# Modulation columns of two chunks summed on VectorE in the head of a two-layer mixer kernel, and conditioning rows made once

## The chip, the cores and the metric

One core of a Trainium2 chip runs the whole program. The metric is the device time of one execution in microseconds (us), the median of several runs. In the profile PE is TensorE's matmul, PEld its weight load, ACT ScalarE, DVE VectorE, POOL GpSimd, and SP the engine that issues most loads; a "q" behind an engine is its instruction queue.

## What is computed

Two layers of a mixer for 384 tokens (128 context tokens, group 0, and 256 latent tokens, group 1) of width 2048, all in float32. Each layer first makes a modulation vector for each group from a conditioning vector, then modulates the normalised input, and then runs projections, attention, a gated MLP, a pooling branch, merge gates and an output projection. Cut to what matters here:

```python
mod_ctx = silu(c_ctx) @ w_ada[l] + b_ada[l]          # 2048 -> 3 * 2048, group 0
mod_lat = silu(c) @ w_ada[l] + b_ada[l]              # the same for group 1
shift, scale, gate = jnp.split(mod, 3, axis=-1)
h = rmsnorm(x, norm_w) * (1.0 + scale) + shift
q, k, v, ga, u, vb, gb, z, gc = split_cols(h @ w_in) # everything else starts from h
```

## The kernel before

Activations lie transposed: 128 channels on the partitions, 384 tokens along the row; a chunk is 128 of the 2048 channels, so a layer has 16 chunks of `h`. A float32 product is made of three fast products: each operand is a rounded high half and the rest (low half). For weights ScalarE rounds the high half `H` (line 75) and VectorE subtracts to get the low half `L` (line 76); for chunks of `h`, ScalarE makes the high half (line 469) and VectorE recomputes and subtracts (lines 470 and 471).

**The stream.** All weights come as 674 tiles of 128 x 1024 (512 KB), in an order that the kernel writes out by hand. Each is an `Item`: it is loaded by SP (line 197), split (`do_split`), multiplied (`mm`), and followed by `post`. `run_items` walks the list; each engine gets its instructions in the order in which this walk issues them, and works them off in that order.

**The head** is the first 92 items of layer 0 (`n_wide`). It has six blocks of token strips `kv` (18 matmuls for two chunks, line 299; here named kv3, kv4 for block 3, kv5, kv6 for block 4), of `t_part` items (24 matmuls, lines 954 to 956, whose results VectorE adds up in line 967), and of modulation items. A modulation strip (`ada_strip`, n chunks wide) multiplies the conditioning columns by `w_ada` on TensorE (line 355) into PSUM; ScalarE copies the result (line 361), TensorE turns it (line 372), and VectorE sums and adds the bias (lines 373 to 380). `ada_pair(c, n)` is the strips of scale and shift for chunks c to c + n - 1. `h` of a chunk can be made only when its pair is done. `nexts` and `SPREAD` say which strips of the next block stand ahead of which item of a block. With n = 4 a strip takes 8 items of 2 matmuls of 512 columns; with n = 2, 4 items of 4 matmuls of 256 columns. The profile records each of these matmuls twice.

In the head an item's split is issued at most two items ahead, and only if at most two splits are open:

```python
while i < n_wide and sp <= i + 2 and sp < loaded[0] and inflight + items[sp].split <= ahead_split:
    if not do_split(items[sp], sp <= i + 1):
        break
```

**Columns on VectorE.** `ada_col` is the other way to get a modulation column: two tiles of transposed `w_ada`, each multiplied with the conditioning row of a group, spread over all partitions in `sB`, and summed by one VectorE instruction (line 399). Layer 0's gates and layer 1's columns are made like this, after the head. The two sums of an item go to the list `lowq`; one is issued after each item with a split, and those of an item that has passed at once:

```python
while lowq and lowq[0][0].idx < i:
    lowq.pop(0)[1]()
...
if it.split and lowq:
    lowq.pop(0)[1]()
```

**Conditioning rows.** `load_cond` (called at item 6 of the part behind the head) loads both rows, spread over 128 partitions, into the four `sb` buffers with POOL's DMA queue. `spread_cond` then applies SiLU to all of it in eight pieces (lines 126 to 128).

**Buffers.** In the head, modulation tiles take one of four `sb` buffers, or else one of up to nine `u` buffers; all other tiles take one of six `raw` buffers (`load_upto`). The SP queue loads in the order of the list, so a tile without a free buffer holds up those behind it. Line 600 scales x by its norm, in parts, at fixed items (26, 48 and 70).

Of the kernel before, what the change touches and what calls it, by code (L numbers as in the profile page):

```python
# [8 lines left out]
F32 = mybir.dt.float32  # L9
F32R = mybir.dt.float32r  # L10
I32 = mybir.dt.int32
AF = mybir.ActivationFunctionType
ALU = mybir.AluOpType
AX = mybir.AxisListType

P = 128
D = 2048
# [12 lines left out]
def hybrid_kernel(ctx: ExitStack, tc: tile.TileContext, x_t, cond_t, cond, vecs_t, cache_kt, cache_v, w_stream,  # L30
                  q_norm_w, k_norm_w, sgu_pool_t, b_sgu, rope_tab, edge_tab, y_t, state_k, state_v, order):
    nc = tc.nc
    PE, ACT, DVE, POOL, SP = nc.tensor, nc.scalar, nc.vector, nc.gpsimd, nc.sync
# [14 lines left out]
    def nm(s):  # L48
        uid[0] += 1
        return f"{s}_{uid[0]}"  # L50

    def unit(dt=F32, shape=(P, 4, T)):
        return big.tile(list(shape), dt, tag="u6", name=nm("u"))

    def s2(shape=(P, 512)):
        return mid.tile(list(shape), F32, tag="s2", name=nm("s"))

    def sm(n):
        return small.tile([P, 16], F32, tag="sm", name=nm("m"))[:, :n]
# [34 lines left out]
    def load_vectors():  # L94
        raw = s2((P, 128))
        SP.dma_start(raw[:, 0:32], cond_t)
        cl = const.tile([P, 2, P], F32, name="cols")
        for l in range(DEPTH):
            v = cl[:, l, :]
            cols.append(dict(norm=v[:, 0:16], ada=v[:, 16:64], merge=v[:, 64:112], pscale=v[:, 112:116],  # L100
                             sguw=v[:, 116:120], fin=v[:, 120:128]))
        sg = s2((P, 128))
        ACT.activation(sg[:, 0:32], raw[:, 0:32], AF.Tanh, scale=0.5)
        DVE.tensor_scalar(sg[:, 0:32], sg[:, 0:32], 0.5, 0.5, ALU.mult, ALU.add)
        for g in range(2):
            DVE.tensor_tensor(scT[:, :, g], sg[:, 16 * g:16 * g + 16], raw[:, 16 * g:16 * g + 16], ALU.mult)
        def vec_load():
            SP.dma_start(cl[:], vecs_t)

        def halve():  # L110
            for c in cols:
                DVE.tensor_scalar(c["merge"], c["merge"], 0.5, None, ALU.mult)
        after(halve, 10)
        ACT.activation(sm(1), eps[:], AF.Ln)
        return vec_load

# [2 lines left out]
    sB = {}  # L119
    scrap = const.tile([P, 1024], mybir.dt.bfloat16, name="scrap")  # L120

    def spread_cond():
        def chunk(g, q):
            sl = sB[g, q // 2][:, (q % 2) * 512:(q % 2 + 1) * 512]
            sg = s2()
            ACT.activation(sg[:], sl, AF.Tanh, scale=0.5)
            DVE.tensor_scalar(sg[:], sg[:], 0.5, 0.5, ALU.mult, ALU.add)
            DVE.tensor_tensor(sl, sl, sg[:], ALU.mult)
        return [lambda g=g, q=q: chunk(g, q) for q in range(4) for g in range(2)]

    def load_cond():
        for g in range(2):
            for hf in range(2):
                sB[g, hf] = sbp.tile([P, 1024], F32, tag="sb", name=nm("sb"))
                POOL.dma_start(sB[g, hf][:], cond[g, hf * 1024:(hf + 1) * 1024].partition_broadcast(P))
    xt_dram = [x_t, tc.dram_tile([4, P, 4, T], F32, name="xt")]


    items = []
# [4 lines left out]
    def after(fn, delay=1):  # L144
        later.setdefault(pos[0] + delay, []).append(fn)
# [21 lines left out]
    loaded = [0]  # L167
    lowq = []
# [3 lines left out]
    def midpoint():  # L172
        while midq:
            midq.pop(0)()

    held = {"sb": 0, "u": 0, "raw": 0}

    def load_upto(n, first=False):
        while loaded[0] < min(n, len(items)):
            it = items[loaded[0]]  # L180
            if it.wide:
                kind = "sb" if first and held["sb"] < 4 else "u"
            else:
                kind = "raw"
            if first and held[kind] >= {"sb": 4, "u": 9, "raw": 6}[kind]:
                return
            held[kind] += 1
            it.kind = kind
            loaded[0] += 1
            if kind == "sb":  # L190
                it.raw = sbp.tile([P, 1024], F32, tag="sb", name=nm("sb"))
            elif kind == "u":
                it.raw = unit(shape=(P, 1024))
            else:
                it.raw = wraw.tile([P, 1024], F32, tag="raw", name=nm("raw"))
            n_col = it.srcs[-1][1]
            SP.dma_start(it.raw[:, :n_col], w_stream[len(order), :, :n_col])
            order.append(it.srcs)
# [18 lines left out]
    def run_items(n_wide, wide_ahead, ahead=5, ahead_split=2):  # L217
# [4 lines left out]
        for i in range(n):  # L222
            while lowq and lowq[0][0].idx < i:
                lowq.pop(0)[1]()
            if i < n_wide:
                load_upto(min(i + 1 + wide_ahead, n_wide + ahead), True)
            else:
                load_upto(i + 1 + ahead)
# [161 lines left out]
    def ada_col(l, c):  # L390
        def mk(hf):
            def pre(it):
                for g in range(2):
                    lowq.append((it, lambda g=g: step(it, g)))

            def step(it, g):
                m = mods[l][:, c, g:g + 1]
                init, dst = ((cols[l]["ada"][:, c:c + 1], part[:, c, g:g + 1]), (part[:, c, g:g + 1], m))[hf]
                DVE.tensor_tensor_reduce(scrap[:], it.raw[:], sB[g, hf][:], 1.0, init,  # L399
                                         ALU.mult, ALU.add, dst)  # L400
                if hf and g:
                    have.add((l, c))
                    if c >= 32:
                        mm = mods[l][:, c, :]
                        DVE.tensor_scalar(mm, mm, 0.25, None, ALU.mult)
                    if 16 <= c < 32:
                        mm = mods[l][:, c, :]
                        DVE.scalar_tensor_tensor(
                            mm, mm, 1.0, cols[l]["norm"][:, c - 16:c - 15].to_broadcast([P, 2]), ALU.add, ALU.mult)
            return pre  # L410

        return [Item([(0, 1024, ("w_ada_t", l), 8 * hf, 8, c * P, P)], pre=mk(hf), split=False) for hf in range(2)]
# [604 lines left out]
    head_a, rest_a = layer(0)  # L1017
# [3 lines left out]
    def ada_pair(c, n):  # L1021
        return ada_strip(0, 16 + c, n) + ada_strip(0, c, n)

    items += ada_pair(0, 1)
    nexts = [ada_pair(1, 1), ada_pair(2, 2)] + [ada_pair(4 * g, 4) for g in range(1, 4)] + [[]]
    SPREAD = [[2, 2, 0], [0, 0, 8], [0, 4, 4, 8], [4, 4, 4, 4, 0, 0], [4, 4, 4, 4, 0, 0], [0, 0, 0, 0, 0, 0]]
    for b in range(6):
        nxt, blk = nexts[b], head_a[b]
        for j, it in enumerate(blk):
            m = SPREAD[b][j]  # L1030
            items += nxt[:m]
            nxt = nxt[m:]
            items.append(it)
        items += nxt
# [1 line left out]
    extra = gate0 + [it for c in range(16) for o in (0, 16) for it in ada_col(1, c + o)]  # L1036
    body, left = mix(rest_a, extra, 2, 20)
    assert not left
    rest_a[6].before = load_cond
    rest_a[12].before = lambda: lowq.extend((rest_a[40], fn) for fn in spread_cond())  # L1040
    items += body
    items += ada_strip(1, 32, 4, 5) + ada_strip(1, 36, 2, 2)
    items += head_b
# [2 lines left out]
    assert not left  # L1046
    items += body
    vec_load = load_vectors()
    xT0 = load_x()
    vec_load()  # L1050
    load_upto(8, True)
    sum_x(xT0)
    run_items(n_wide, 24)
# [75 lines left out]
```

## Time and profile before

| | before |
|---|---|
| median of 3 runs (lowest to highest) | 2159.76 us (2159.47 to 2160.26) |
| the profiled execution | 2159.66 us, span 2157.9 us |
| granted TensorE clock, mean | 0.997 |
| TensorE busy | 2136.8 us (99%) |
| VectorE busy | 1290.1 us (60%) |
| ScalarE busy | 790.9 us (37%) |
| share of the chain that ended last | TensorE 99%, VectorE 1% |
| TensorE line 355 (modulation strips) in that chain | 2% |
| DMA moved | 375.60 MB |

The span runs from the first to the last instruction of the trace; the time is that of the whole execution. The chain is followed back from the last instruction, at each step to what released it. A line that is idle elsewhere costs nothing as long as it is not in this chain.

### The profile page before, as it was taken

The page shows a single profiled execution, that of the slowest core. Times are in us where ns is not written, and L with a number is a line of the kernel's source. Part 1 is how long each engine was busy: PE and PEld are TensorE (multiplying, and loading weights), DVE is VectorE, ACT ScalarE, POOL GpSimd, SP SyncE. Part 2 cuts the span into 40 slices and gives each one's busy share as a digit, 9 for nine tenths or more (in the row PEclk, how much of TensorE's full clock was granted, in tenths as well). Part 3 has the DMA queues.
Part 4 walks back from the last instruction along what each step waited for, and adds up shares of the span by engine and source line. Part 5 has one row for each costly group of instructions (what it writes and reads, how often), then busy time and mean ns, then how long its engine had stood idle before and what let it go on. Part 6 is the DMA issues. An engine that isn't in the chain of part 4 may idle for free.

```text
span 2157.9 us, 30028 instructions
## 1 busy us (share of the span) xinstructions
PE 2136.8 (99%) x12102; PEld 2027.6 (94%) x12102; DVE 1290.1 (60%) x2015; ACT 790.9 (37%) x1137; POOL 22.6 (1%) x70
## 2 busy tenths in 40 slices
PE   8999999999999999999999999999999999999997
PEld 6789898989999999999988889999999999999997
DVE  6566775757667876767767676753443444443444
ACT  4242445453323333333344345453232333332432
POOL 0000000000000000000000000000000000000000
PEclk9999999999999999999999999999999999999998
DMA  9965354545555565567774553443333333334531
GB/s 383 409 216 187 119 185 148 175 143 183 197 190 184 189 196 188 184 200 240 254 256 142 163 165 128 161 143 108 127 125 129 127 127 127 126 126 135 176 128 72
DMA packets 104461, 375.60 MB, mean 174 GB/s; under 512 B 11937, under 2 KB 13473, under 8 KB 104321
## 3 DMA queue, kind: packets, MB, share of 16 engines
q1 hardware_dynamic: 101056, 359.66, 49.4%
q0 software_dynamic: 3264, 14.03, 2.1%
q8 instruction: 94, 1.54, 0.3%
q14 instruction: 47, 0.38, 0.1%
HBM read 366.82 MB, written 6.82 MB: 173 GB/s over the span
## 4 chain that ended last, share of the span: by engine, by line
PE 99%; DVE 1%; ACT 0%; DMA 0%; issue 0%; DVEq 0%; SPq 0%
PE b L336 26%; PE b L334 26%; PE b L335 26%; PE b L279 3%; PE b L278 3%; PE b L277 3%; PE b L299 3%; PE b L355 2%; PE b L954 1%; PE b L562 1%; PE b L542 1%; PE b L956 1%; PE b L955 1%; PE b L553 1%; PE b L589 0%; DVE u L1014 0%
## 5 line engine op out<-in xcount | busy, mean ns | idle before, releaser
L334 PE MATMUL b<-u,H 128*128 128x384 f32 x3184 | 1075.7, 338 | 0.0
L336 PE MATMUL b<-u,L 128*128 128x384 f32 x3184 | 1064.2, 334 | 0.0
L335 PE MATMUL b<-u,H 128*128 128x384 f32 x3184 | 1063.9, 334 | 0.0
L76 DVE TENSOR_TENSOR L<-raw,H 128x1024 fp32r<-128x1024 f32 (+1 forms) x481 | 587.0, 1221 | 638.1 <-ACT H L75 638.0
L75 ACT ACTIVATE H<-raw 128x1024 fp32r<-128x1024 f32 (+1 forms) x481 | 507.2, 1055 | 838.0 <-PE b L335 686.4
L335 PEld LDWEIGHTS b<-u,H 128*128 128x128 f32 x3184 | 597.9, 188 | 4.5 <-issue 1.0
L334 PEld LDWEIGHTS b<-u,H 128*128 128x128 f32 x3184 | 597.9, 188 | 4.5 <-issue 1.0
L336 PEld LDWEIGHTS b<-u,L 128*128 128x128 f32 x3184 | 597.7, 188 | 0.0
L399 DVE CUSTOM_DVE_ANT_0 scrap<-raw,sb,part 128x1024 bf16<-128x1024 f32 x116 | 148.2, 1277 | 0.0
L399 DVE CUSTOM_DVE_ANT_0 scrap<-raw,sb,cols 128x1024 bf16<-128x1024 f32 x116 | 148.1, 1276 | 0.0
L277 PE MATMUL b<-H,u 128*128 128x512 f32 x288 | 115.1, 400 | 0.0
L279 PE MATMUL b<-H,u 128*128 128x512 f32 x288 | 112.4, 390 | 0.0
L278 PE MATMUL b<-L,u 128*128 128x512 f32 x288 | 112.2, 390 | 0.0
L832 ACT ACTIVATE s<-b,cols 128x384 f32<-128x384 f32 x96 | 55.6, 581 | 114.4 <-PE b L336 114.4
L278 PEld LDWEIGHTS b<-L,u 128*128 128x128 f32 x288 | 54.1, 188 | 11.8
L277 PEld LDWEIGHTS b<-H,u 128*128 128x128 f32 x288 | 54.1, 188 | 11.7
L279 PEld LDWEIGHTS b<-H,u 128*128 128x128 f32 x288 | 54.0, 188 | 11.5
L299 PE MATMUL b<-H,u 128*128 128x512 f32 x192 | 52.8, 397 | 0.2 <-DVE u L471 0.2
L954 PE MATMUL b<-u,H 128*128 128x384 f32 x144 | 49.7, 345 | 0.0
L956 PE MATMUL b<-u,L 128*128 128x384 f32 x144 | 48.4, 336 | 0.0
L955 PE MATMUL b<-u,H 128*128 128x384 f32 x144 | 48.2, 335 | 0.0
L846 DVE SCALAR_TENSOR_TENSOR s<-s,b 128x384 f32<-128x384 f32 x64 | 35.4, 552 | 20.0 <-PE b L336 20.0
(165 smaller groups left out, 1138.8 us busy)
## 6 DMA issues: line engine op xcount, KB each, us to landing
raw<-in_w_stream_dram SPq DMA_DIRECT2D x594, 512.0 KB, 3.3
u<-in_w_stream_dram SPq DMA_DIRECT2D x56, 512.0 KB, 10.1
sb<-in_w_stream_dram SPq DMA_DIRECT2D x20, 512.0 KB, 10.2
u<-in_x_t_dram SPq DMA_DIRECT2D x8, 384.0 KB, 6.0
u<-in_x_t_dram POOLq DMA_DIRECT2D x8, 384.0 KB, 5.9
xt<-u POOLq DMA_DIRECT2D x4, 768.0 KB, 5.4
u<-xt POOLq DMA_DIRECT2D x8, 384.0 KB, 3.9
out_dram<-u SPq DMA_DIRECT2D x6, 384.0 KB, 2.7
```

Source lines behind the costliest of these rows:

```text
L75: ACT.activation(dst_h, src, AF.Copy)
L76: DVE.tensor_tensor(dst_l, src, dst_h.bitcast(F32), ALU.subtract)
L277: PE.matmul(ps, lh, rh, start=first, stop=False)
L278: PE.matmul(ps, lh, rl, start=False, stop=False)
L279: PE.matmul(ps, ll, rh, start=False, stop=last)
L299: PE.matmul(st["ps"][t][:], hslice(h[a], kk, t), b[:, cs], start=(kk == 0 and q == 0), stop=(kk == 15 and q == 2))
L334: PE.matmul(ps, wh, rh, start=(kk == 4 * i0), stop=False)
L335: PE.matmul(ps, wh, rl, start=False, stop=False)
L336: PE.matmul(ps, wl, rh, start=False, stop=(kk == 4 * n_p - 1))
L399: DVE.tensor_tensor_reduce(scrap[:], it.raw[:], sB[g, hf][:], 1.0, init, ALU.mult, ALU.add, dst)
L954: PE.matmul(ps[n][:, :T], wh, rh, start=(k == 0), stop=False)
L956: PE.matmul(ps[n][:, :T], wl, rh, start=False, stop=(k == nk - 1))
```

## The change

`ada_pair(12, 4)` becomes `ada_pair(12, 2)`: the modulation strips for chunks 12 to 15 shrink to chunks 12 and 13. The scale and shift columns of chunks 14 and 15 are made as `ada_col` items: eight tiles of 128 x 1024, four of them put into block 3 (one ahead of each of its t_parts) and four into block 4 (one ahead of each of its first four items). The number of tiles in the stream stays 674, that of the head 92.

For that `sB` must be there by block 3. `load_cond` moves to the first token strip of block 3; from that block's first item on, modulation tiles no longer take `sb` buffers. The SiLU of the conditioning rows is made once, by `save_cond` at item 12, on 32 rows of 128 numbers, and stored in DRAM; `load_cond` spreads the result from there. `spread_cond` is gone.

```diff
@@ -111,6 +111,7 @@
             for c in cols:
                 DVE.tensor_scalar(c["merge"], c["merge"], 0.5, None, ALU.mult)
         after(halve, 10)
+        after(save_cond, 12)
         ACT.activation(sm(1), eps[:], AF.Ln)
         return vec_load
 
@@ -119,20 +120,22 @@
     sB = {}
     scrap = const.tile([P, 1024], mybir.dt.bfloat16, name="scrap")
 
-    def spread_cond():
-        def chunk(g, q):
-            sl = sB[g, q // 2][:, (q % 2) * 512:(q % 2 + 1) * 512]
-            sg = s2()
-            ACT.activation(sg[:], sl, AF.Tanh, scale=0.5)
-            DVE.tensor_scalar(sg[:], sg[:], 0.5, 0.5, ALU.mult, ALU.add)
-            DVE.tensor_tensor(sl, sl, sg[:], ALU.mult)
-        return [lambda g=g, q=q: chunk(g, q) for q in range(4) for g in range(2)]
+    cond_s = tc.dram_tile([2, D], F32, name="cs")
+
+    def save_cond():
+        rows = "g (k p) -> (g k) p"
+        c, sg = s2()[0:32, 0:P], s2()[0:32, 0:P]
+        POOL.dma_start(c, cond.rearrange(rows, p=P))
+        ACT.activation(sg, c, AF.Tanh, scale=0.5)
+        DVE.tensor_scalar(sg, sg, 0.5, 0.5, ALU.mult, ALU.add)
+        DVE.tensor_tensor(c, c, sg, ALU.mult)
+        POOL.dma_start(cond_s.rearrange(rows, p=P), c)
 
     def load_cond():
         for g in range(2):
             for hf in range(2):
                 sB[g, hf] = sbp.tile([P, 1024], F32, tag="sb", name=nm("sb"))
-                POOL.dma_start(sB[g, hf][:], cond[g, hf * 1024:(hf + 1) * 1024].partition_broadcast(P))
+                POOL.dma_start(sB[g, hf][:], cond_s[g, hf * 1024:(hf + 1) * 1024].partition_broadcast(P))
     xt_dram = [x_t, tc.dram_tile([4, P, 4, T], F32, name="xt")]
 
 
@@ -173,13 +176,14 @@
         while midq:
             midq.pop(0)()
 
+    no_sb = [0]
     held = {"sb": 0, "u": 0, "raw": 0}
 
     def load_upto(n, first=False):
         while loaded[0] < min(n, len(items)):
             it = items[loaded[0]]
             if it.wide:
-                kind = "sb" if first and held["sb"] < 4 else "u"
+                kind = "sb" if first and held["sb"] < 4 and loaded[0] < no_sb[0] else "u"
             else:
                 kind = "raw"
             if first and held[kind] >= {"sb": 4, "u": 9, "raw": 6}[kind]:
@@ -1022,11 +1026,22 @@
         return ada_strip(0, 16 + c, n) + ada_strip(0, c, n)
 
     items += ada_pair(0, 1)
-    nexts = [ada_pair(1, 1), ada_pair(2, 2)] + [ada_pair(4 * g, 4) for g in range(1, 4)] + [[]]
-    SPREAD = [[2, 2, 0], [0, 0, 8], [0, 4, 4, 8], [4, 4, 4, 4, 0, 0], [4, 4, 4, 4, 0, 0], [0, 0, 0, 0, 0, 0]]
+    nexts = [ada_pair(1, 1), ada_pair(2, 2)] + [ada_pair(4, 4), ada_pair(8, 4), ada_pair(12, 2)] + [[]]
+
+    def cols_of_chunk(c):
+        return ada_col(0, 16 + c) + ada_col(0, c)
+
+    direct = {3: cols_of_chunk(14), 4: cols_of_chunk(15)}
+    SPREAD = [[2, 2, 0], [0, 0, 8], [0, 4, 4, 8], [4, 4, 4, 4, 0, 0], [2, 2, 2, 2, 0, 0], [0, 0, 0, 0, 0, 0]]
     for b in range(6):
         nxt, blk = nexts[b], head_a[b]
         for j, it in enumerate(blk):
+            if b == 3 and j == 0:
+                it.before = load_cond
+                no_sb[0] = len(items)
+            if b in direct and (b == 4 or j >= 2):
+                items += direct[b][:1]
+                direct[b] = direct[b][1:]
             m = SPREAD[b][j]
             items += nxt[:m]
             nxt = nxt[m:]
@@ -1036,8 +1051,6 @@
     extra = gate0 + [it for c in range(16) for o in (0, 16) for it in ada_col(1, c + o)]
     body, left = mix(rest_a, extra, 2, 20)
     assert not left
-    rest_a[6].before = load_cond
-    rest_a[12].before = lambda: lowq.extend((rest_a[40], fn) for fn in spread_cond())
     items += body
     items += ada_strip(1, 32, 4, 5) + ada_strip(1, 36, 2, 2)
     items += head_b
```

## Rows read from the trace of the kernel before

**Rows 1.** Busy time by engine, 60 to 100 us; then clock, DMA share, GB/s.

```profile
60.00:100.00 40.00, 40.00 (x252) 28.59 (x253) 22.01 (x42) 13.08 (x19) 0.00 (x0) 1.00 1.03 409
```

**Rows 2.** TensorE's instructions in order: start, us, line, operands, count.

```profile
38.04 2.37 PE L355 MATMUL b<-u,scT 128*32 128x256 f32 x40
65.52 1.90 PE L355 MATMUL b<-sb,scT 128*32 128x512 f32 x16
107.11 1.92 PE L355 MATMUL b<-u,scT 128*32 128x512 f32 x16
108.96 1.02 PE L299 MATMUL b<-H,u 128*128 128x512 f32 x3
109.81 0.85 PE L299 MATMUL b<-L,u 128*128 128x512 f32 x3
113.31 1.93 PE L355 MATMUL b<-sb,scT 128*32 128x512 f32 x16
117.37 0.60 PE L372 MATMUL b<-ident,s 128*128 128x128 f32 x4
117.73 0.94 PE L299 MATMUL b<-H,u 128*128 128x512 f32 x3
121.83 0.45 PE L954 MATMUL b<-u,H 128*128 128x384 f32 x1
```

**Rows 3.** DMA issues, whole run: KB of one, median us to landing.

```profile
sb<-in_cond_dram POOLq DMA_DIRECT2D x4, 512.0 KB, 12.1
```

**Rows 4.** DMA queues from 173 to 179 us: packets, MB, share.

```profile
q0 software_dynamic: 343, 1.25, 51.5%
q1 hardware_dynamic: 332, 1.22, 49.8%
```

**Rows 5.** All engines in order, around the weights of block 3.

```profile
78.26 1.06 ACT L75 ACTIVATE H<-raw 128x1024 fp32r<-128x1024 f32 x1 [3.59 <-DMA raw<-in_w_stream_dram]
81.09 0.53 PEld L299 LDWEIGHTS b<-H,u 128*128 128x128 f32 x3 [0.84 <-ACT u L469]
84.60 1.06 ACT L75 ACTIVATE H<-raw 128x1024 fp32r<-128x1024 f32 x1 [2.71 <-DMA raw<-in_w_stream_dram]
```

**Rows 6.** The chain that ended last, in order: start, us, engine, line.

```profile
87.82 0.38 PE b L954
```

**Rows 7.** VectorE's groups by shape, 60 to 150 us.

```profile
L76 DVE TENSOR_TENSOR L<-raw,H 128x1024 fp32r<-128x1024 f32 x16 | 19.5, 1221 | 5.7 <-ACT H L75 5.7
L967 DVE TENSOR_TENSOR u<-u,b 128x384 f32<-128x384 f32 x24 | 13.2, 553 | 26.9 <-PE b L956 26.9
L471 DVE TENSOR_TENSOR u<-s,u 128x384 fp32r<-128x384 f32 x12 | 6.7, 559 | 1.4 <-DMA sb<-in_w_stream_dram 0.2 <-ACT u L469 0.2
L470 DVE TENSOR_SCALAR s<-u,mods 128x256 f32<-128x256 f32 x12 | 4.9, 407 | 0.0
L470 DVE TENSOR_SCALAR s<-u,mods 128x128 f32<-128x128 f32 x12 | 4.1, 342 | 0.0
L600 DVE TENSOR_TENSOR u<-u,s 128x1536 f32<-128x1536 f32 x2 | 3.5, 1752 | 0.0
```

**Rows 8.** VectorE's groups by shape, whole run: one weighted sum.

```profile
L399 DVE CUSTOM_DVE_ANT_0 scrap<-raw,sb,part 128x1024 bf16<-128x1024 f32 x116 | 148.2, 1277 | 0.0
```

**Rows 9.** All engines in order: a low half, and who waits for it.

```profile
34.00 0.19 PEld L956 LDWEIGHTS b<-u,L 128*128 128x128 f32 x1 [0.36 <-DVE L L76]
...
107.21 0.55 DVE L967 TENSOR_TENSOR u<-u,b 128x384 f32<-128x384 f32 x1 [1.53 <-PE b L956]
107.69 1.22 DVE L76 TENSOR_TENSOR L<-raw,H 128x1024 fp32r<-128x1024 f32 x1
```

**Rows 10.** ScalarE in order: where the conditioning rows would be made.

```profile
40.04 0.38 ACT L361 ACTIVATE s<-b 128x256 f32<-128x256 f32 x1 [8.08 <-PE b L355]
```

**Rows 11.** VectorE's groups, 0 to 400 us: part of `spread_cond`.

```profile
L128 DVE TENSOR_TENSOR sb<-sb,s 128x512 f32<-128x512 f32 x8 | 5.5, 692 | 0.3
```

## The prediction

> **What bounds the kernel now.** I read the chain that ended last first: nearly all of it is TensorE, so a microsecond counts only if it moves TensorE. In the busy times from 60 to 100 us TensorE is busy in all 40 us, VectorE in 22, and the DMA engines are full at 409 GB/s [rows 1]. That mean hides three limits that lie close together, so I read the stretch in order. The weights of kv3 and kv4 (the first two token strips of block 3) come from the DMA just in time: ScalarE waits 3.59 us for kv4's weights and starts the high half at 78.26 us; TensorE starts kv4 at 81.09 us, released by ScalarE [rows 5]. VectorE, half idle on average, works in program order: at 34.00 us TensorE waits for a low half that VectorE makes only after copies that had to wait for TensorE [rows 9]. After the head TensorE never waits long, so what the last head matmul is moved by, the end is moved by. The profiled execution took 2159.66 us (span 2157.9), 0.10 us under the median; I add to it.
>
> **What TensorE is spared.** Four 512-wide strip items (16 records) take 1.85 us, from 107.11 to 108.96 us; 256-wide, 40 records take 2.37 us, so 16 take 0.95 [rows 2]. Block 4 had 16 wide items in four groups, 7.4 us; it gets 8 narrow ones, 3.8 us: 3.6 us saved. Four transposes fewer save 0.36 us (117.37 to 117.73 us) [rows 2]. Together **-4.0 us**, and no more is to be had, since TensorE has hardly a gap elsewhere. Eight streamed loads replace eight: the bytes of the stream stay.
>
> **The broadcast load, moved into the full DMA.** `load_cond` goes from the body into block 3: four loads of 512 KB, 2.10 MB, 5.1 us at 409 GB/s [rows 1, 3]. Its issuer, POOL, has only `save_cond` ahead of it, and the four `sb` buffers are free once TensorE has left the strip items that use them, by 67.4 us [rows 2]. So it runs beside the weights of kv3 and kv4. From 173 to 179 us, where the same load met the weight queue, each queue had half of the engines (51.5% and 49.8%) [rows 4]. Hence about 10 us at half rate, from some 68 to 78 us, and everything streamed behind it lands 5.1 us later. kv4 has little to give: high half 1.06 us plus two activations of about 0.5 each after 78.26 us makes 80.3, TensorE started at 81.09 [rows 5]; of 5.1 us, **+4.3 us** arrive. Bounds: 0 if the stream has more lead than I read, 5.1 if none. I take the upper part, because ScalarE is seen waiting on precisely these loads. The next weights lie one load (1.28 us at 409 GB/s) further back, behind the first direct item: 6.4 us later, against a high half started at 84.60 us, low half done 1.06 + 1.22 later at 86.88, needed at 87.82 + 0.45 [rows 2, 5 to 7]: slack 1.39. As TensorE is already 4.3 late, **+0.7 us** more.
>
> The SP queue also loses four `sb` buffers for strips of blocks 3 and 4, and direct items take six-deep `raw` buffers. I cost both at nothing: from the later half of block 3 the loads gain on TensorE, and six `raw` tiles still span three or four splits.
>
> **The weighted sums, in front of the splits.** Eight direct items give 16 sums of 1.28 us [rows 8], 20.4 us on VectorE, which is 18 us idle in the 40 us of rows 1; by share they fit. But an item's first sum is issued behind the previous split item, its second at the next item, and the next split only two items ahead, so a pair (2.55 us) stands between VectorE's adds for one item and the low half (1.22) of the next. The last add (0.55) cannot start before that item ends on TensorE; at 107.21 us it does so, the low half follows [rows 7, 9]. Before, four wide strips (1.85 us) lay there as cover; now there are two narrow ones (0.95 us), or, between t_parts of block 3, none. The third matmul of a t_part needs the low half, 0.45 us in [rows 2]; a kv item needs it after 0.85 us, and its corrected `h` chunk after another 0.70, while that chunk costs VectorE 0.34 + 0.41 + 0.56 = 1.31 [rows 2, 7]. Stalls, each as VectorE's work less TensorE's cover:
> - second t_part of block 3: 0.55 + 2.55 + 1.22 - 1.85 - 0.45 = 2.0
> - third and fourth (low half behind the adds, before the sums): 0.55 + 1.22 - 0.45 = 1.3 each
> - kv5: 0.55 + 2.55 + 1.22 - 0.95 - 0.85 = 2.5, and 1.31 - 0.70 = 0.6 for the chunk: 3.1
> - kv6, counted from kv5's low half: two chunks 2.62, the scaling of line 600 1.75, sums 2.55, low half 1.22 = 8.1; TensorE the rest of kv5 (113.31 - 108.96 - 0.85 = 3.5), 0.6, 0.95, 0.85 = 5.9: 2.2, and 0.6: 2.8
> - first t_part of block 4, from kv6's low half: 2.62 + 2.55 + 1.22 = 6.4 against 3.5 + 0.6 + 0.2 + 0.95 + 0.45 = 5.7: 0.7
> - second: 0.55 + 2.55 + 1.22 - 0.95 - 0.45 = 2.9
>
> The sum is 14.1; neighbouring VectorE instructions overlap by some 0.08 us (107.21 + 0.55 against 107.69), about 1 us over eight places: **+13.1 us**. Bounds: 0, if the queue always has the low halves done before, to 20.4, if every sum shows in full. I take the worked value, as the rows nearest to it (34.00 and 107.21 us) show both the order and the wait.
>
> **Without price.** `save_cond`'s small loads, one Tanh, two VectorE operations and a store fall into ScalarE's 8.08 us of waiting before 40.04 us [rows 10]; what they could cost, if the load landed late, is the wait of ScalarE behind it, a few us at most and only with a landing as late as the 12.1 us of a 512 KB load [rows 3]. The removed `spread_cond` (eight products of 0.69 us and what goes with them [rows 11]) ran beside a TensorE without waits: nothing comes back.
>
> Sum: -4.0 + 4.3 + 0.7 + 13.1 = +14.1; 2159.66 + 14.1 = **2173.8 us**.
>
> **A rule against the row.** POOL issued these four loads at once before, and the slower half of them landed after 12.1 us or more [rows 3]; the sums need them some 20 us after 67.4. "GPSIMD Engine Reference" of the Trainium skill, 1. Specifications, says that POOL shares its SBUF interfaces with VectorE and contends with VectorE instructions that read two SBUF inputs. By that rule POOL could be held while writing the descriptors of this load, as VectorE's splits and sums are of that kind; no run here shows it yet. It is the fifth rival.
>
> **The rivals.**
> 1. *Forecast*: broadcast and sums both show. 2173.8.
> 2. *Sums alone*: the weight stream has lead enough. -4.0 + 13.1 + some of the slack: 2169. For it: kv4 waited under 1 us on TensorE. Against: the DMA is full through 100 us [rows 1].
> 3. *Not slower, the idle VectorE takes the sums* and only the broadcast shows: -4.0 + 5.0 = 2160.7. The mechanism is the 18 us idle of rows 1; it decides if the low halves are done ahead of the sums, so that a pair meets a VectorE that would have waited. Against: at most one t_part of the t_parts and kv items concerned has its split issued ahead.
> 4. *Both hidden*: 2159.66 - 4.0 = 2155.7, the best possible.
> 5. *The broadcast lands later than the first sums*: VectorE waits in order, and the low half of the next t_part behind it. The point is a landing over 20 us after issue; each us beyond costs one. With 5 us: 2179. That is slower for another reason.
> 6. *The change does not do what it says*, the narrow strips costing as much as the wide ones: 4 us more, 2178. The row of 256-wide strips speaks against it [rows 2].
>
> **How the numbers follow.** Chances: 0.50, 0.14, 0.13, 0.13, 0.07, 0.03. A measurement of this kernel can tell about 0.2%, 4.3 us, from no change. Faster by more: 0.03, a part of rival 4, whose gain lies at this bound. Within: rival 3 and the rest of 4, 0.23. Slower: 0.74. The range leaves out most of rival 4 and of 5: 2157 to 2179; it holds both ends of the broadcast's price and the sums from 0 to a third more than worked out.
>
> **What would show it.** Right: TensorE's wait list names VectorE's line 76 as releaser for lines 954, 955, 956 and 299 between 90 and 150 us, some 13 us in all; the start of kv4 moves by about 4 us; block 5 starts near 155 us, not 141. Wrong: TensorE without gaps in block 4, low halves done before the adds, or the broadcast landing before 70 us without moving the weights of kv3 and kv4; also any change behind 300 us.

## Result and profile after

The changed kernel took 2180.31 us (median; 2178.30 to 2182.34), the kernel before beside it 2159.91 us (2159.47 to 2160.26): a ratio of 1.0094 [1.0083, 1.0106], 20.4 us slower. The forecast was 2173.8 us with a range up to 2179: direction and places right, size 6.5 us too small. The profiled execution took 2180.27 us, 20.6 more than that of before; 20.3 of it lie in the span. From line 180 of the new file on, lines stand four further down than before (L303 was 299, L359 355, L365 361, L376 372, L403 399, L473 to L475 469 to 471, L958 to L960 954 to 956, L971 967).

The page of after: span, busy times, and the chain that ended last by engine.

```profile
span 2178.2 us, 30043 instructions
...
PE 2141.6 (98%) x12098; PEld 2030.1 (93%) x12098; DVE 1303.5 (60%) x2035; ACT 786.0 (36%) x1130; POOL 23.4 (1%) x72
...
PE 93%; DVE 1%; DMA 0%; issue 0%; ACT 0%; DVEq 0%; ACTq 0%
```

VectorE has 13 us more to do and still 60% of the span. The shares say nothing of 20 us; the waits do. TensorE's waits of after, 80 to 165 us (waiting line and releaser: total, times, longest):

```profile
PE b L960 <- DVE L L76: 7.6, 4, 2.8
PE b L303 <- DVE L L76: 4.3, 2, 2.4
PE b L303 <- ACT u L473: 1.8, 1, 1.8
PE b L303 <- DVE u L475: 0.5, 2, 0.3
PE b L359 <- DMA u<-in_w_stream_dram: 0.5, 1, 0.5
```

11.9 us go to VectorE's low halves, 2.3 to kv4's late weights. These are the waits that the prediction named, but together 14.7 us, not 20. The rest shows only in TensorE's rows read in order. Timeline of TensorE, after (start, duration, what, and in brackets the wait before it):

```profile
81.57 1.05 PE L359 MATMUL b<-u,scT 128*32 128x512 f32 x4 [0.54 <-DMA u<-in_w_stream_dram]
84.42 1.23 PE L303 MATMUL b<-H,u 128*128 128x512 f32 x3 [1.79 <-ACT u L473]
85.48 1.44 PE L303 MATMUL b<-L,u 128*128 128x512 f32 x3
...
99.77 0.34 PE L959 MATMUL b<-u,H 128*128 128x384 f32 x1
102.10 0.44 PE L960 MATMUL b<-u,L 128*128 128x384 f32 x1 [2.00 <-DVE L L76]
103.16 0.52 PE L958 MATMUL b<-u,H 128*128 128x384 f32 x1
...
106.49 0.33 PE L958 MATMUL b<-u,H 128*128 128x384 f32 x1
...
108.23 0.34 PE L959 MATMUL b<-u,H 128*128 128x384 f32 x1
110.00 0.44 PE L960 MATMUL b<-u,L 128*128 128x384 f32 x1 [1.43 <-DVE L L76]
...
119.93 1.07 PE L359 MATMUL b<-u,scT 128*32 128x256 f32 x16
120.93 0.96 PE L303 MATMUL b<-H,u 128*128 128x512 f32 x3
124.31 0.96 PE L303 MATMUL b<-L,u 128*128 128x512 f32 x3 [2.42 <-DVE L L76]
...
132.34 0.96 PE L303 MATMUL b<-L,u 128*128 128x512 f32 x3 [1.86 <-DVE L L76]
133.58 1.65 PE L303 MATMUL b<-H,u 128*128 128x512 f32 x3 [0.28 <-DVE u L475]
...
148.40 0.44 PE L960 MATMUL b<-u,L 128*128 128x384 f32 x1 [2.77 <-DVE L L76]
...
160.89 0.86 PE L303 MATMUL b<-H,u 128*128 128x512 f32 x3
```

The same matmul on line 958 takes 0.52 us at 103.16 and 0.33 us at 106.49. The first is not waiting for anything: it runs at half the clock. The busy times by stretch, after (length, PE, PEld, DVE, ACT, POOL busy, granted clock, DMA share, GB/s), show where:

```profile
86.00:90.00 4.00, 4.00 (x15) 3.10 (x14) 2.46 (x8) 0.21 (x1) 0.00 (x0) 0.63 1.02 409
90.00:98.00 8.00, 8.00 (x53) 5.27 (x56) 4.31 (x7) 1.06 (x1) 0.00 (x0) 1.00 1.03 409
...
102.00:106.00 4.00, 3.90 (x15) 3.80 (x16) 0.05 (x1) 1.06 (x1) 0.00 (x0) 0.57 0.98 376
...
134.00:138.00 4.00, 4.00 (x14) 2.99 (x13) 2.87 (x8) 0.00 (x0) 0.00 (x0) 0.66 0.35 112
```

From 102 to 106 us TensorE is busy in 3.90 of 4 us, yet gets 15 records done where before had 25: the granted clock is 0.57, that is, mostly 1.2 instead of 2.4 GHz. In before the clock is 1.00 in all stretches from 82 to 154 us. In the profiled run of after it fell three times, each time right behind a wait of TensorE (those before 84.42, 102.10 and 132.34). Behind the longer waits before 124.31 and 148.40 it did not fall.

With the start of each item in both traces, the 20 us split up (before, after, growth of the shift between the two; "add" is the last add of line 971 for that item; kv5, kv6, t5 and t6 are counted without the strips ahead of them, which have a row of their own):

| up to | before | after | growth | forecast |
|---|---|---|---|---|
| kv4 | 81.09 | 84.42 | +3.33 | broadcast, in all to t2: |
| strips behind kv4 | 85.90 | 91.04 | +1.81 (1.1 of it clock) | |
| t2 (second t_part of block 3) | 93.97 | 99.49 | +0.38 | +5.0, measured +5.52 |
| add of t2 | 98.89 | 108.25 | +3.84 | +2.0 |
| add of t3 | 103.05 | 114.15 | +1.74 | +1.3 |
| add of t4 | 107.21 | 120.04 | +1.73 | +1.3 |
| kv5, to its end | 113.31 | 128.49 | +3.21 | +3.1 |
| kv6, to its end | 119.97 | 138.22 | +3.93 | +2.8 less 0.18 (transposes) |
| t5, to its end | 126.19 | 144.01 | +0.43 | +0.7 |
| add of t6 | 132.96 | 152.77 | +2.85 | +2.9 less 0.18 (transposes) |
| four strip groups between these | | | -3.44 | -3.6 |
| block 5 (kv7) | 141.09 | 160.89 | +19.80 in all | +14.1 |

The 1.1 us of clock behind kv4 come from the next section: with the broadcast alone the clock stayed up, and the same stretch grew by 0.7 us.

Behind block 5 the shift grows by 0.5 us more: the last stores are issued 20.0 us later than in before (2166.99 and 2147.02 us), and 0.3 us lie behind their issue. What makes them I have not found; TensorE's waits behind 200 us are those of before.

The DMA queues, after, 66 to 82 us (packets, MB, share of 16 engines), and the load's issue (count, size, median us to landing):

```profile
q1 hardware_dynamic: 1207, 4.41, 69.3%
q0 software_dynamic: 576, 2.10, 32.7%
...
sb<-cs POOLq DMA_DIRECT2D x4, 512.0 KB, 10.8
```

The broadcast is there as predicted, 2.10 MB beside kv3's and kv4's weights, though it took a third of the engines and not the half of [rows 4]. That it is this load that makes kv4 late, and not the four buffers that the stream lost, shows in the issue of kv4's weights on SP (the first line before, the others after) and in ScalarE's high half:

```profile
67.34 0.33 SPq L197 DMA_DIRECT2D raw<-in_w_stream_dram  x1
67.50 1.62 SPq L201 DMA_DIRECT2D raw<-in_w_stream_dram  x2
82.92 1.06 ACT L75 ACTIVATE H<-raw 128x1024 fp32r<-128x1024 f32 x1 [8.40 <-DMA raw<-in_w_stream_dram]
```

The weights are asked for 0.16 us later than in before, and ScalarE can start on them 4.66 us later (82.92 against 78.26): the time went by on the shared DMA engines.

### The profile page after: what moved, and what is told of

Same layout as the page of the kernel before. It is cut to its first block, busy times and chain, and to the rows that moved or that the text cites. A ratio compares the mean times of both kernels' runs of the same rounds, so it can differ in the third digit from the quotient of the medians.

```text
span 2178.2 us, 30043 instructions
## 1 busy us (share of the span) xinstructions
PE 2141.6 (98%) x12098; PEld 2030.1 (93%) x12098; DVE 1303.5 (60%) x2035; ACT 786.0 (36%) x1130; POOL 23.4 (1%) x72
## 4 chain that ended last, share of the span: by engine, by line
PE 93%; DVE 1%; DMA 0%; issue 0%; ACT 0%; DVEq 0%; ACTq 0%
PE b L340 25%; PE b L338 25%; PE b L339 25%; PE b L283 3%; PE b L282 3%; PE b L281 3%; PE b L303 2%; PE b L566 1%; PE b L546 1%; PE b L557 1%; PE b L960 1%; PE b L959 0%; PE b L958 0%; DMA raw<-in_w_stream_dram 0%; DVE u L1018 0%; PE b L481 0%
## 5 line engine op out<-in xcount | busy, mean ns | idle before, releaser
L403 DVE CUSTOM_DVE_ANT_0 scrap<-raw,sb,part 128x1024 bf16<-128x1024 f32 x124 | 158.6, 1279 | 0.1
L403 DVE CUSTOM_DVE_ANT_0 scrap<-raw,sb,cols 128x1024 bf16<-128x1024 f32 x124 | 158.5, 1278 | 0.1
L281 PEld LDWEIGHTS b<-H,u 128*128 128x128 f32 x288 | 54.1, 188 | 11.7
L283 PEld LDWEIGHTS b<-H,u 128*128 128x128 f32 x288 | 54.1, 188 | 11.4
L303 PE MATMUL b<-H,u 128*128 128x512 f32 x192 | 55.2, 410 | 2.6 <-ACT u L473 1.8
L960 PE MATMUL b<-u,L 128*128 128x384 f32 x144 | 49.7, 345 | 7.8 <-DVE L L76 7.6
L958 PE MATMUL b<-u,H 128*128 128x384 f32 x144 | 50.2, 349 | 0.1
L303 PEld LDWEIGHTS b<-H,u 128*128 128x128 f32 x192 | 36.1, 195 | 14.1 <-ACT u L473 4.9
```

Of the source, the lines that this page charges most:

```text
L281: PE.matmul(ps, lh, rh, start=first, stop=False)
L283: PE.matmul(ps, ll, rh, start=False, stop=last)
L303: PE.matmul(st["ps"][t][:], hslice(h[a], kk, t), b[:, cs], start=(kk == 0 and q == 0), stop=(kk == 15 and q == 2))
L960: PE.matmul(ps[n][:, :T], wl, rh, start=False, stop=(k == nk - 1))
```

## The experiments

**The broadcast alone.** All modulation columns on TensorE as before, the conditioning rows made once and loaded in block 3.

```diff
-    nexts = [ada_pair(1, 1), ada_pair(2, 2)] + [ada_pair(4, 4), ada_pair(8, 4), ada_pair(12, 2)] + [[]]
+    nexts = [ada_pair(1, 1), ada_pair(2, 2)] + [ada_pair(4 * g, 4) for g in range(1, 4)] + [[]]
-    direct = {3: cols_of_chunk(14), 4: cols_of_chunk(15)}
+    direct = {}
```

> The changed kernel without its direct items and with wide strips for chunks 12 to 15 as before; only the conditioning rows are made early and spread in block 3. Theory (late weights + low halves behind the sums + clock): kv4 starts 3.4 us later as in the changed kernel, one fall of the clock costs up to 1.8 us more, no wait on VectorE's line 76 behind sums: 2163 to 2166 us. Rival A (the broadcast is hidden, all of the loss is VectorE's): 2160. Rival B (the broadcast carries the unexplained 5 us too): over 2168.

2164.97 us, 1.0026 [1.0016, 1.0036]: +5.2, as expected. (A difference with a sign is against the kernel before, as it ran beside that version.) Its TensorE waits, 15 to 165 us:

```profile
PE b L303 <- ACT u L473: 1.8, 1, 1.8
PE b L359 <- DMA u<-in_w_stream_dram: 0.9, 1, 0.9
PE b L303 <- DVE u L475: 0.4, 2, 0.2
```

The clock stays at 1.00 here, although kv4 waits as long for ScalarE (1.76 us, until 84.79) as in after. kv4 starts 3.7 us later than in before, and from there to the strips behind it 5.52 us pass, 0.7 more than before: a wait of 0.2 us for VectorE and slower first matmuls behind both waits. In after the same stretch took 6.62 us, so the fall of the clock cost 1.1 us there. From the strips to t2 nothing is added, and block 5 starts 4.4 us late.

**The same load, one block later**: `b == 3` becomes `b == 4` in the line that sets `it.before = load_cond`.

> The kernel of the broadcast alone, with the broadcast one block later: the strips of block 3 keep their four buffers, and the four loads start when these are free, near 92 us, when the weights have lead on TensorE. Theory (the 5 us come from the place, where weights land just in time): 2159 to 2161 us. Rival (a broadcast of 2.10 MB costs its 5 us anywhere while the DMA is full): 2164 to 2166.

2160.91 us, 1.0004 [0.9995, 1.0013], as expected. POOL issues at 81.61 and 87.35 us, and the same 2.10 MB cost 1.0 us instead of 5.2, an amount that the interval does not tell from nothing; one wait of 0.32 us is left for line 76. The DMA engines are as full there (share 1.03 from 82 to 118 us), so the place costs, not the bytes. The edit also lets the strips of block 3 keep their `sb` buffers; that these weigh little shows in the broadcast alone, where kv4's weights are issued 0.55 us later than in before (67.89 us), but land 5 us later.

**The sums alone.** The kernel before with narrow strips and the direct items; the sums multiply each tile by itself, as no spread rows are there yet.

```diff
-                DVE.tensor_tensor_reduce(scrap[:], it.raw[:], sB[g, hf][:], 1.0, init,
+                DVE.tensor_tensor_reduce(scrap[:], it.raw[:], (sB[g, hf] if sB else it.raw)[:], 1.0, init,
```

> The kernel before with narrow strips and the direct items in blocks 3 and 4, whose sums multiply each tile with itself instead of the conditioning row, so that the broadcast can stay where it was, behind the head; the columns of chunks 14 and 15 are therefore other numbers. Theory: strips -3.8, waits for low halves +13 to +14, kv4 not late, up to two falls of the clock at 1.7 each: 2169 to 2173 us. Rival A (without the broadcast VectorE's idle time takes the sums): 2156 to 2158. Rival B (the whole loss is VectorE's): 2180.

2174.70 us, 1.0068 [1.0053, 1.0083]: +14.9, 1.7 us over the upper end of what I expected. TensorE's waits, 90 to 165 us:

```profile
PE b L956 <- DVE L L76: 7.5, 4, 2.8
PE b L299 <- DVE L L76: 4.3, 2, 2.4
...
```

They are the waits of after to 0.1 us, with kv4 on time. +5.2 and +14.9 make 20.1 of the 20.4 us: the two parts add up, and rivals 2, 3 and 4 are out.

**The strips alone.** The kernel before with chunks 14 and 15 left out altogether (their columns are set to 1).

> The kernel before with narrow strips for chunks 12 and 13 only, and nothing in place of the columns of chunks 14 and 15 (they stay at 1, and eight tiles are not loaded); conditioning rows as before. It measures the gain alone. Theory: 8 narrow strip items and four transposes fewer, -3.8 us: 2155.5 to 2156.5 us. Rival (other waits take the place): 2158 or more.

2157.02 us, 0.9987 [0.9977, 0.9996]: -2.9, where the prediction had -4.0; my expectation of 2155.5 to 2156.5 was 0.5 us too low at its upper end. TensorE's waits, 15 to 165 us (L301 and L958 are 299 and 954 of before):

```profile
PE b L301 <- DVE u L473: 0.5, 2, 0.3
PE b L958 <- DVE L L76: 0.2, 1, 0.2
```

The narrow groups are as short as forecast (119.93 to 120.93 us in after, 1.00 instead of 1.85), but 0.7 us of waits for VectorE stand in the list, where before had 0.2: the longer strips had covered the rest, and each new wait brings a slower first matmul with it. Rival 6 is out; the term was too large by 1.1 us by itself. With this gain taken out, the sums by themselves cost 14.9 + 2.9 = 17.8 us. In after, the stalls in the table hold these waits already.

**The order.** After, with the split issued up to five items ahead instead of two:

```diff
-            while i < n_wide and sp <= i + 2 and sp < loaded[0] and inflight + items[sp].split <= ahead_split:
+            while i < n_wide and sp <= i + 5 and sp < loaded[0] and inflight + items[sp].split <= ahead_split:
```

> The changed kernel with splits in the head issued up to five items ahead instead of two (still at most two open). Theory: the low half of the third and fourth t_part of block 3 is issued ahead of the adds of the one before (2.9 us less), those of kv5, kv6 and the second t_part of block 4 ahead of at least one pair of sums (some 5 us less), with fewer falls of the clock; kv4 stays late: 2166 to 2172 us. Rival (VectorE's load, not its order, decides): within 2 us of the changed kernel, 2178 to 2182.

2168.09 us, 1.0039 [1.0024, 1.0054]: the 16 sums are all there, 12.2 of the 20.4 us are gone. But a wait is new, at 25.66 us, in the first block (L372, 368 of before, for ScalarE's line 365: 2.13 us). To see what the edit does by itself, the same in the kernel before:

> The kernel before with splits in the head issued up to five items ahead instead of two. It tells whether the gain of that edit on the changed kernel is owed to the sums. Theory (no low half is late before): 2159 to 2160.5 us. Rival (it helps by itself): 2156 or less.

2163.58 us, 1.0017 [1.0008, 1.0027]: +3.7, with a new wait of TensorE of 2.42 us at 26.19 us; my expectation of no harm was wrong. ScalarE, before, with the edit (start, duration, what, the wait before it):

```profile
25.35 0.63 ACT L75 ACTIVATE H<-raw 128x512 fp32r<-128x512 f32 x1 [3.23 <-DMA raw<-in_w_stream_dram]
25.88 0.26 ACT L361 ACTIVATE s<-b 128x128 f32<-128x128 f32 x1
```

A split issued early puts ScalarE's high half, whose tile has not landed, ahead of the small copy of line 361 that TensorE needs. It is the same fault as that of the change, on another engine: ready work queued behind work that isn't ready. So the look-ahead of five was then confined to items from 42 on (`5 if i >= 42 else 2`):

> The changed kernel with splits up to five items ahead from block 3 on only, so that the first blocks stay as they were (there the same edit made TensorE wait 2.4 us for ScalarE). Theory (the place of the sums in VectorE's order makes the waits for low halves; what stays is the broadcast among the weights of kv3 and kv4): 2163 to 2166 us, the level of the broadcast alone, or below it by part of the 2.9 us that the strips spare. Rival (VectorE has too much to do from block 3 on): no better than 2167.

2167.25 us, 1.0034 [1.0021, 1.0046]: +7.5. TensorE's waits, 15 to 165 us:

```profile
PE b L960 <- DVE L L76: 2.6, 2, 2.0
PE b L303 <- ACT u L473: 1.8, 1, 1.8
...
```

One number in a condition takes back 13.1 us, with all sums left in: most of the loss was VectorE's order. (Sparing the first block gave only 0.8 us of it: with that block late, kv4 waited 0.9 instead of 1.8 us for ScalarE.) But 2.3 us more than the broadcast alone remain, 1.25 over my upper end, and the rival's number (no better than 2167) is met. What is left is a wait of 2.00 us at 129.16 us and two stretches of lower clock (0.79 from 82 to 90, 0.72 from 128 to 134 us). From 110 to 134 us VectorE is busy in 23.09 of 24 us, and at 125.15 and 126.47 us two sums again stand ahead of the low half that TensorE waits for: there the load of the sums counts too, and these runs do not separate it from the order. Net of the broadcast and of the strips' gain, the sums still cost about 7.5 - 5.2 + 2.9 = 5.2 us, of 17.8.

**The clock.** After, with 43 unused 128-column matmuls placed ahead of the items that wait:

```diff
+    fill = {51: 6, 63: 6, 65: 4, 67: 4, 71: 8, 75: 6, 83: 9}
...
+            if i in fill:
+                idle = bank()
+                for _ in range(fill[i]):
+                    PE.matmul(idle[:, 0:P], ones[:], ident[:], start=True, stop=True)
```

> The changed kernel with 43 matmuls of 128 columns that nothing uses on TensorE, 4 to 9 of them (0.29 us each, 12.5 us in all) ahead of kv4, kv5, kv6 and four t_parts, where it waited 1.4 to 2.8 us. Theory (falls of the clock cost about 5 us): granted clock 1.00 from 80 to 150 us, and, as the added work fits into the waits, 2174 to 2177 us, faster than the changed kernel though TensorE does more. Rival (the falls cost nothing, TensorE waits for VectorE anyway): 2180 or more.

2177.08 us (2176.39 to 2177.64), 1.0081 [1.0064, 1.0098]: 0.1 us over the upper end of what I expected, and no run as long as the shortest of after (2178.30). The busy times by stretch:

```profile
82.00:90.00 8.00, 7.53 (x38) 5.03 (x34) 5.34 (x13) 3.30 (x6) 0.00 (x0) 1.00 1.03 410
98.00:108.00 10.00, 8.68 (x63) 7.18 (x55) 6.11 (x12) 3.66 (x4) 0.00 (x0) 1.00 0.92 359
124.00:138.00 14.00, 12.47 (x83) 8.47 (x82) 12.44 (x22) 2.39 (x3) 0.00 (x0) 1.00 0.58 203
```

The unused matmuls by themselves, in the same view (PE and PEld busy, clock, DMA share, GB/s):

```profile
80.00:165.00 85.00, 11.24 (x86) 10.26 (x86) 1.00 0.74 273
```

TensorE does 11.2 us more and the kernel is 3.2 us faster: the clock stays at 1.00 in all three places. From kv4's start to the strips behind it 5.50 us pass (84.51 to 90.01 us), as in the broadcast alone, against 6.62 in after. So the three falls cost some 3 us more than the fill does. By the table they cost 4.2 us, 1.1 behind kv4 and 3.1 at t2 and kv6 (worked out below); the fill doesn't fit each gap exactly (TensorE still waits 0.5 to 0.8 us behind it), so neither figure is good to a tenth.

**Less on VectorE.** Three versions that might have kept the gain of the narrow strips, all with `load_cond` at the fifth item of block 3. First, chunk 15 alone on VectorE, its items in block 4, and look-ahead five everywhere:

```diff
-    direct = {3: cols_of_chunk(14), 4: cols_of_chunk(15)}
+    direct = {4: cols_of_chunk(15)}
```

> The direct columns for chunk 15 alone, four direct items in block 4 from its third item on, strips two wide for chunks 12 and 13 and one wide for chunk 14, the broadcast one block later, and splits up to five items ahead. Theory: strips -1.8 us, the broadcast nothing, 8 sums (10.2 us) in a stretch where VectorE has more idle time than that and splits stand ahead of them, waits 0 to 2 us: 2157.5 to 2160 us, no measurable loss. Rival (any sum in the head delays low halves): 2163 or more.

2163.70 us, 1.0017 [1.0008, 1.0025]; missed, with the wait in the first block again (2.30 us at 25.90 us). The same with look-ahead five from item 42 on:

> The one-chunk version with splits up to five items ahead from block 3 on only. Theory: without the 2.4 us wait in the first block, 2159 to 2161 us: the strips' 1.5 us and what the late broadcast and the last waits for kv8 cost cancel. Rival (the one-chunk version gains when the first block is left alone): 2158 or less.

2161.42 us, 1.0007 [0.9998, 1.0016]: 0.4 us over my upper end, and not the rival's gain. Its TensorE waits, 15 to 165 us:

```profile
PE b L960 <- DVE L L76: 0.6, 1, 0.6
PE b L303 <- DVE u L475: 0.5, 2, 0.3
PE b L303 <- DVE L L76: 0.3, 1, 0.3
```

Nearly nothing waits, and still nothing is won over before. Block 5 starts on time (141.15 us, 141.09 in before); its second strip then waits 0.35 and 0.28 us, behind the last pair of sums (141.72 and 143.05 us), and is done 1.2 us late. Last, both chunks in block 4, two items ahead of its second to fifth:

> Both chunks' direct items in block 4, two ahead of each of its second to fifth items, the broadcast one block later, splits up to five items ahead from block 3 on. Theory (in block 4 alone VectorE then has some 38 us of work, 19 of its own and 16 sums, against 30 of TensorE): waits of 5 to 8 us, 2162 to 2166 us. Rival (order alone decides, load does not): strips -2.9 and broadcast +1.0, 2157 to 2159.

2164.34 us, 1.0020 [1.0011, 1.0030], as expected; TensorE's waits for line 76 add up to 4.6 us although the clock doesn't fall. From 124 to 138 us VectorE is busy in 13.75 of 14 us: here it is VectorE's load more than its order. No version with the sums was faster than the kernel before.

## Why the prediction was right in kind and wrong in size

*What bounds the kernel*: right. Every microsecond that TensorE lost in the head was lost at the end (19.8 of 20.3 by block 5).

*The broadcast, +4.3 and +0.7*: the sum is right (+5.2 alone, +5.5 in after), and so is its first step, but part of it is luck. ScalarE got kv4's weights late, and kv4 started 3.7 us later alone and 3.3 in after, instead of 4.3. The +0.7 for the next weights didn't come: alone, nothing is added between the strips behind kv4 and t2. In its place kv4 itself took 0.7 us longer behind its waits, and in after the fall of the clock cost 1.1, which I had not thought of. That the load met these weights is shown by their issue and landing, and by the later place (+1.0).

*The strips, -4.0*: the durations were right; the term left out that the longer strips had covered work of VectorE, for which TensorE then waits (-2.9 alone).

*The sums, +13.1*: the step that failed; they cost 17.8 us by themselves (14.9 with the strips' gain) and 18.1 in after by the table. The mechanism is shown: the wait list names line 76 at the places forecast, with 11.9 us in all, and issuing splits earlier takes 13.1 us back. So the waits came out as worked out, and what lies around them was mis-sized, in two ways. VectorE, after, around the third t_part:

```profile
108.25 0.55 DVE L971 TENSOR_TENSOR u<-u,b 128x384 f32<-128x384 f32 x1 [1.23 <-PE b L960]
108.72 1.22 DVE L76 TENSOR_TENSOR L<-raw,H 128x1024 fp32r<-128x1024 f32 x1
109.86 1.28 DVE L403 CUSTOM_DVE_ANT_0 scrap<-raw,sb,cols 128x1024 bf16<-128x1024 f32 x1
```

First, the hand-overs. The add, the low half, then the matmul is the order that I had in [rows 7, 9]. TensorE's last matmul ahead of the stall starts at 108.23 us, and the next would have followed 0.17 us later, at 108.40; it came at 110.00, and its successor 0.28 instead of 0.17 us after it: 1.71 us, where I had 1.3. The add starts 0.2 us behind t3's first matmul (108.05), when t2's last one has drained; the first matmul after the stall adds 0.1; and the cover ahead of the low half was 0.35 us, not 0.45, as no strip stands ahead of t3. I had no term for the first two, and subtracted 1 us for overlap instead. Without the clock, the stalls of the table are 15.0 us (17.7, plus 0.4 for the transposes, less 3.1 for the two falls at t2 and kv6, whose waits explain 2.3 of 3.84 and 2.6 of 4.1), against 13.1: 1.9 us.

Second, the clock. It was no term and no rival, with a granted clock of 1.00 in [rows 1], and it is the larger part: 3.1 us by the table at t2 and kv6. The fill, which took away these two falls and the one behind kv4, gave back 3.2 us net. Stalls 1.9 and clock 3.1, with 0.5 from the broadcast, 0.2 from the strips and 0.5 behind block 5, are all of the 6.2 us within the span that were missing (0.3 more lie outside it). How the 1.9 split at the other stalls I did not work out.

One reading behind this term was wrong, too: at 34.00 us [rows 9] it is the weight load that waits 0.36 us. The matmul itself came only 0.2 us late, and VectorE had been busy without a break, not waiting for TensorE, since 30.82 us. The row showed the order, but hardly a cost.

*The range* took in the sums up to a third more (17.4 us); they cost 18.1, and it ended 1.3 us too low. The clock also goes with the spread of after's runs, 4 us where before's is less than 1: the run of 2178.30 us had a mean clock of 0.996, that of 2182.34 us 0.993, those in between 0.994. That the number of falls differs from run to run would fit; only one run of each kernel has a trace, so it isn't shown.

*The other rivals.* Rivals 2, 3, 4 and 6 fall with the runs above. Rival 5 as well: VectorE's first sum starts at 89.65 us, 23 us after the issue at 66.79, without a wait; the slowest quarter of the load had landed after 13.8. POOL wrote its four issues in 2.13 us. The Trainium skill's rule of the shared interface ("GPSIMD Engine Reference", 1. Specifications) can hold and yet decide nothing here: no run shows POOL held up. *Without price* was right: TensorE has no wait near `save_cond`, and ScalarE has its wait before 40 us as in [rows 10].

## What to carry to other kernels

An operation put on a half-idle engine costs what is queued behind it, not what it takes: look for the conversion that another engine needs next, and issue that first; but a look-ahead that is too long queues ready work behind data that hasn't landed, and where the engine has hardly any idle time left (23.09 of 24 us busy with the confined look-ahead), order has little more to give. Price each new wait of TensorE with its hand-over (some 0.3 us here: 0.2 for the drain and 0.1 for the first matmul) and with a lower clock behind it. A bulk load belongs where the stream has lead: 2.1 MB cost 5.2 us in one block and at most about 1 us in the next.

## What the runs showed of the hardware

Short waits can cost TensorE twice. Behind waits of some 2 us in a busy stretch the granted clock fell to the lower level (1.2 GHz), three times in the profiled run of after, once in that of the sums alone, twice in that with the confined look-ahead, and unused matmuls in the waits made the kernel 3.2 us faster. The length of the wait alone doesn't decide: 1.76 us before kv4 left the clock alone in one kernel, 1.77 us at the same place lowered it in another, and 2.77 us before 148.40 us in after did nothing. The Trainium skill ("TensorE: Matmul & The Clock Gate", Part 1) says that the low clock is the default and that activity releases it; the traces agree so far as every fall stands behind idle time and none came where fill took its place. What picks the waits that lead to a fall stays open.
